# Streaming the high and low halves of the activations in one 512-column matmul, with groups of two channel tiles, in a one-core hybrid decoder layer

## The chip, the cores and the metric

The program runs on one core of a Trainium2 chip. The metric is device time of one launch in microseconds. The kernel before takes 532.43 us, the median of three runs that lie between 532.12 and 532.71 us.

## What is computed

One layer of a decoder for 256 tokens of width 2048, in float32:

```
h = rms_norm(x);  p = h @ w_in          # w_in is 2048 x 6408
A: RG-LRU (512 channels): conv4, gates, h_t = a_t h_{t-1} + u_t, times silu(lru_z)
B: mLSTM (768 channels): conv4, silu, block-diagonal q/k/v, gated scores, layer norm, times silu(ml_z)
C: attention (768 channels, 6 heads of 128, one causal block, ALiBi), times silu(mo_z)
x = x + concat(A, B, C) @ w_out
x = x + cross_attention(rms_norm(x), rms_norm(mem)) @ xa_wo      # 4 heads of 128
out = rms_norm(x)
```

## The kernel before

**The big products as split products.** `w_in`, `w_out`, `xa_wkv`, `xa_wq` and `xa_wo` come through one stream of 172 chunks, numbered from 0 (`CHUNKS`). A chunk is 128 partitions by up to 1024 columns of weights (512 KB). `load` (L151) brings it into one of four `raw` buffers, and `split` (L166) makes of it a high part `wh` on ACT (a copy that rounds to fp32r, L188) and a low part `wl` on DVE (raw minus high, L139), each in six buffers. The activations have a high and a low part too, in separate tiles `ah` and `al` (L196). A product is three fp32r matmuls: high by high, high by low, low by high.

**Groups.** `GROUPS` (L42) lists the passes over the contraction (16 tiles of 128). A group of kind `W` keeps weights stationary and streams 256 token columns; its result is [channel, token], two channel tiles side by side in each of two PSUM banks, so four channel tiles in a group. A chunk of it has two contraction tiles by four channel tiles, so 8 pairs of three matmuls:

```
 250 P.matmul(o, h[:, sl], mv_h, start=first and m % 2 == 0, stop=False, ...)
 251 P.matmul(o, h[:, sl], mv_l, start=False, stop=False, ...)
 253     P.matmul(o, l[:, sl], mv_h, start=False, stop=last, ...)
```

Kind `X` keeps activations stationary and streams 384 to 512 weight columns (L265 to L267). PSUM holds four accumulator banks (two groups) and four `ps` banks for all other matmuls.

**The order of the work** is written out (L1009 on). For chunk i the program first splits up to chunk i + 4 (`SPLIT_AHEAD`), then issues `mm(i)`, and when i ends a group calls `done` (L958), and then takes one `step` (L925) from a queue of generators. `done` puts the read-out of the finished accumulators at the head of the queue (`urgent`) and longer work at its end (`bg`): the recurrence (`lru_core`, L421), the mLSTM convolution (`ml_conv`, L486), gates, heads (L581) and layer norm (`ml_norm`, L636), and the attention heads (`mo_heads`, L697). Each engine runs its instructions in program order, so a read-out that waits for PE also holds the splits queued behind it on its engine, and each urgent read-out takes the step of one chunk from the work behind it. The step after chunk i stands on DVE and ACT just ahead of the split of chunk i + 5.

**Read-outs.** A bank holds two channel tiles. `silu_evac` (L458) multiplies the bank by the row of inverse norms on DVE and applies Silu on ACT; `u_evac` (L479), `qk_evac` (L684) and `ck_evac` (L800) are the multiplication alone, and `cq_evac` (L806) two ACT copies.

**Places that the prediction speaks of.** Chunks 16 to 23 are group `u1` (the last two tiles of u, the first two of lru_z), 24 to 39 are `o0` and `o1` (kind `X`), 40 to 79 are `q0`, `q1`, `k0`, `k1`, `z0`, 80 to 95 are `v0`, `v1` (kind `X`), 96 to 107 are `z1`, `z2`, 108 to 139 the output projection, 140 to 155 `ck` and `cq`, 156 to 163 `cv`. In `lru_core` the gate matmuls are L432 and L433, their sigmoids L434 and L435, the Exp and Tanh of the decays L440 and L441, the square root L448, the scan L454. In `ml_norm` the statistics are L642 and L643, the power on POOL L646, the scaling L652, the transposes on PE L660.

Of the kernel before, what the change touches and what calls it, by code (L numbers as in the profile page):

```python
# [18 lines left out]
NK = D // 128  # L19
# [7 lines left out]
# column offsets in w_in  # L27
# [10 lines left out]
def _t(off, *tiles):  # L38
# [22 lines left out]
    ("ck", "xa_wkv", "W", "m", _cols(0, 128, 256, 384)),  # L61
    ("cq", "xa_wq", "W", "h", _cols(0, 128, 256, 384)),
# [7 lines left out]
# per-partition vectors: name -> columns  # L70
# [27 lines left out]
def kernel(ctx: ExitStack, tc: tile.TileContext, xT, memT, x, mem, ws, vec_d, lw_d, fg_d, out):  # L98
# [16 lines left out]
    # ------------------------------------------------------------------ helpers  # L115
# [28 lines left out]
    # ------------------------------------------------------------------ weight stream  # L144
# [21 lines left out]
    def split(i, part=(0, 1)):  # L166
# [14 lines left out]
        elif GROUPS[g][0] == "cq":  # L181
            for kk in range(2):
                sl = slice(kk * n, (kk + 1) * n)
                gk = vc("xa_g", 2 * j + kk)
                S.activation(h[:, sl], r[:, sl], AF.Copy, scale=gk)
                stt(l[:, sl], r[:, sl], gk, h[:, sl].bitcast(F32), OP.mult, OP.subtract)
# [5 lines left out]
    # ------------------------------------------------------------------ activations  # L192
    act_hi = {"x": [None] * 8, "y": [None] * 8, "m": [None] * 8, "h": [None] * 8, "c": [None] * 2}
    act_lo = {"x": [None] * 8, "y": [None] * 8, "m": [None] * 8, "h": [None] * 8, "c": [None] * 2}

    def act_pair(which, j):  # L196
        tag = "y" if which in "ym" else "x"
        h = acts.tile([128, 512], F32R, tag="h" + tag, name=f"ah_{which}{j}")
        l = acts.tile([128, 512], F32R, tag="l" + tag, name=f"al_{which}{j}")
        act_hi[which][j], act_lo[which][j] = h, l  # L200
        return h, l
# [23 lines left out]
    def split_pair(which, j, src):
        """hi and lo of a [128, 512] float32 pair of contraction tiles."""
        h, l = act_pair(which, j)
        S.activation(h, src, AF.Copy)
        tt(l, src, h.bitcast(F32), OP.subtract)

    # ------------------------------------------------------------------ matmuls of the stream
    acc = {}

    def mm(i):
# [6 lines left out]
        for kk in range(kc):  # L241
            k = kc * j + kk
            xh, xl = act_hi[act][k // 2], act_lo[act][k // 2]
            first, last, b = k == 0, k == NK - 1, k % 2 * 256
            if kind == "W":
                mv_h, mv_l = xh[:, b:b + 256], xl[:, b:b + 256]
# [11 lines left out]
            else:  # L258
                mh, ml = h[:, kk * n:kk * n + n], l[:, kk * n:kk * n + n]
                for t in range(2):  # L260
# [3 lines left out]
                    sl = slice(b + t * 128, b + t * 128 + 128)  # L264
# [4 lines left out]
        if name == "cv" and j == 7:  # L269
            for t in range(2):  # L270
                for kk in range(2):
                    sl = slice(kk * 256 + t * 128, kk * 256 + t * 128 + 128)
                    P.matmul(a[t], xh[:, sl], h[:, kk * n:kk * n + n], start=False, stop=False)
                    P.matmul(a[t], xh[:, sl], l[:, kk * n:kk * n + n], start=False, stop=False)
                    P.matmul(a[t], xl[:, sl], h[:, kk * n:kk * n + n], start=False, stop=kk == 1)

    # ------------------------------------------------------------------ start: loads and constants
# [37 lines left out]
    def late_consts():  # L315
# [5 lines left out]
        # the product of the q and k blocks, transposed: the sum over o of wq[c, o] wk[d, o]  # L321
# [14 lines left out]
    def rstd_of(out_t, ssq, n, eps):  # L336
        """out = (ssq / n + eps) ** -0.5"""
# [4 lines left out]
    def log1p(out_t, e, name):  # L342
        """log(1 + e) for 0 <= e <= 1 as 2 artanh(e / (2 + e))"""
# [25 lines left out]
    # ------------------------------------------------------------------ row statistics  # L369
# [4 lines left out]
    def square(which, j):  # L374
        """adds the squares of a pair of staged contraction tiles to the running sum"""
# [34 lines left out]
    # ------------------------------------------------------------------ RG-LRU  # L410
# [51 lines left out]
    def lru_z(a, b, c):  # L462
        if c == 0:
            L["sz"] = big(1, 4, 256)
        silu_evac(L["sz"][:, c:c + 2, :], a, b)
        yield
# [9 lines left out]
    # ------------------------------------------------------------------ mLSTM  # L476
    M = {}

    def u_evac(a, b, c):  # L479
# [3 lines left out]
        tt(M["u"][:, c:c + 2, 3:259], bank(a, b), rb("x"), OP.mult)  # L483
# [182 lines left out]
    def ml_z(a, b, c):  # L666
        if c == 0:
            M["sz"] = big(6, 6, 256)
        silu_evac(M["sz"][:, c:c + 2, :], a, b)
        yield  # L670
# [10 lines left out]
    # ------------------------------------------------------------------ MoBA: one causal block  # L681
    B = {}

    def qk_evac(which, tag, a, b, c):  # L684
        if c == 0:
            B[which] = big(tag, 6, 256)
        tt(B[which][:, c:c + 2, :], bank(a, b), rb("x"), OP.mult)
# [75 lines left out]
    # ------------------------------------------------------------------ residual and norm before cross-attention  # L763
# [36 lines left out]
    def ck_evac(a):  # L800
        C["k"] = big(1, 4, 256)
        for b in range(2):
            tt(C["k"][:, 2 * b:2 * b + 2, :], bank(a, b), rb("m"), OP.mult)
        yield

    def cq_evac(a):  # L806
        qT = big(2, 4, 256)
        for b in range(2):
            S.activation(qT[:, 2 * b:2 * b + 2, :], bank(a, b), AF.Copy)
# [32 lines left out]

    def cv_out(a):
# [9 lines left out]
        for t in range(2):  # L853
# [4 lines left out]
            oh, ol = act_pair("c", t)  # L858
# [5 lines left out]
    # ------------------------------------------------------------------ output projection and final norm  # L864
# [247 lines left out]
```

## Time and profile before

| what | value |
|---|---|
| median of the timed runs | 532.43 us (532.12 to 532.71) |
| profiled execution, first to last instruction (its own time; the page gives no other) | 530.7 us |
| what lies around that span in the timed runs | 1.7 us (532.43 - 530.7) |
| PE, PEld busy | 519.7 and 486.1 us |
| DVE, ACT, POOL busy | 339.3, 281.4 and 49.7 us |
| DMA | 96.73 MB, 182 GB/s |

How to read it: PE is the matmul side of the tensor engine and PEld its weight loads, which overlap. A matmul's listed duration contains its way through the pipeline, so that matmuls overlap in the records; what one costs in a stream is the distance from its start to the next one's start. The chain of work that ended last follows the end of the kernel back to what released each step.

### The profile page before, as it was taken

The numbers are of one execution on the slowest core, as the hardware profiler recorded it, in microseconds if no ns is written. First come the engines' busy times: TensorE is split into PE (matmuls) and PEld (weight loads), VectorE is DVE, ScalarE is ACT, GpSimd is POOL, SyncE is SP. The second block draws the span as 40 slices with busy tenths as digits, with TensorE's granted clock in tenths as the row PEclk, the third lists the DMA queues.
The fourth block names the chain that finished last, engine by engine and source line by source line (L and its number), as shares of the span: only waits on it lengthen the run. The fifth ranks groups of instructions, "written<-read, shape, count | busy, mean of one in ns | idle before, by whom it ended". The sixth has DMA issues, their size and how long they took to land.

```text
span 530.7 us, 8855 instructions
## 1 busy us (share of the span) xinstructions
PE 519.7 (98%) x3498; PEld 486.1 (92%) x3498; DVE 339.3 (64%) x520; ACT 281.4 (53%) x419; POOL 49.7 (9%) x62
## 2 busy tenths in 40 slices
PE   8999999999999999999999999999999999999993
PEld 6999999999998889999999999888888899998883
DVE  6986927794576435466657667665667875437574
ACT  5964477577644232342456455553657665347343
POOL 7462000200000000000200000000051110000000
PEclk9999999999999999999999999999999999999997
DMA  8985535468455445535367335688685555633604
GB/s 286 357 262 178 149 113 174 127 201 269 136 185 162 131 143 165 160 100 178 120 186 255 116 120 167 200 298 278 215 286 184 171 189 190 207 117 115 220 24 158
DMA packets 30362, 96.73 MB, mean 182 GB/s; under 512 B 3312, under 2 KB 3696, under 8 KB 30320
## 3 DMA queue, kind: packets, MB, share of 16 engines
q1 hardware_dynamic: 30176, 96.02, 55.3%
q8 instruction: 27, 0.44, 0.3%
q14 instruction: 15, 0.12, 0.1%
q10 hardware_dynamic: 144, 0.14, 0.1%
HBM read 94.05 MB, written 2.10 MB: 181 GB/s over the span
## 4 chain that ended last, share of the span: by engine, by line
PE 93%; issue 2%; DMA 2%; DVE 2%; SPq 0%; ACT 0%; ACTq 0%; POOLq 0%; POOL 0%; DVEq 0%
PE acc_out L265 6%; PE acc_out L267 5%; PE acc_out L266 5%; PE acc_z L253 4%; PE acc_z L251 4%; PE acc_z L250 4%; PE acc_k L250 3%; PE acc_q L250 3%; PE acc_u L250 3%; PE acc_u L253 3%; PE acc_u L251 3%; PE acc_k L251 3%; PE acc_q L251 3%; PE acc_q L253 3%; PE acc_k L253 3%; PE acc_o L266 2%
## 5 line engine op out<-in xcount | busy, mean ns | idle before, releaser
L139 DVE TENSOR_TENSOR wl<-raw,wh 128x1024 fp32r<-128x1024 f32 (+3 forms) x166 | 197.9, 1203 | 100.0 <-ACT wh L188 99.2
L188 ACT ACTIVATE wh<-raw 128x1024 fp32r<-128x1024 f32 (+2 forms) x162 | 161.1, 1010 | 55.5 <-PE acc_k L251 12.8
L265 PE MATMUL acc_out<-wh,ah_y 128*128 128x512 f32 x128 | 50.8, 397 | 0.0
L267 PE MATMUL acc_out<-wh,al_y 128*128 128x512 f32 x128 | 49.9, 390 | 0.0
L266 PE MATMUL acc_out<-wl,ah_y 128*128 128x512 f32 x128 | 49.8, 389 | 0.0
L250 PE MATMUL acc_z<-ah_x,wh 128*128 128x256 f32 x160 | 46.6, 291 | 0.0
L253 PE MATMUL acc_z<-ah_x,wl 128*128 128x256 f32 x160 | 45.2, 283 | 0.0
L251 PE MATMUL acc_z<-al_x,wh 128*128 128x256 f32 x160 | 45.2, 283 | 0.0
L250 PE MATMUL acc_q<-ah_x,wh 128*128 128x256 f32 x128 | 37.2, 291 | 0.0
L250 PE MATMUL acc_k<-ah_x,wh 128*128 128x256 f32 x128 | 37.0, 289 | 0.0
L250 PE MATMUL acc_u<-ah_x,wh 128*128 128x256 f32 x128 | 36.8, 288 | 0.0
L383 POOL TENSOR_TENSOR mask<-mask,yt 128x512 f32<-128x512 f32 x14 | 22.3, 1594 | 150.7 <-ACT yt L382 150.7
L253 PE MATMUL acc_u<-ah_x,wl 128*128 128x256 f32 x128 | 36.2, 283 | 0.0
L251 PE MATMUL acc_k<-al_x,wh 128*128 128x256 f32 x128 | 36.2, 283 | 0.0
L251 PE MATMUL acc_u<-al_x,wh 128*128 128x256 f32 x128 | 36.2, 283 | 0.0
L253 PE MATMUL acc_q<-ah_x,wl 128*128 128x256 f32 x128 | 36.2, 283 | 0.0
L251 PE MATMUL acc_q<-al_x,wh 128*128 128x256 f32 x128 | 36.2, 283 | 0.0
L253 PE MATMUL acc_k<-ah_x,wl 128*128 128x256 f32 x128 | 36.2, 283 | 0.0
L251 PEld LDWEIGHTS acc_z<-al_x,wh 128*128 128x128 f32 x160 | 30.6, 192 | 0.2
L250 PEld LDWEIGHTS acc_z<-ah_x,wh 128*128 128x128 f32 x160 | 30.6, 192 | 0.2
L253 PEld LDWEIGHTS acc_z<-ah_x,wl 128*128 128x128 f32 x160 | 30.6, 191 | 0.0
L267 PEld LDWEIGHTS acc_out<-wh,al_y 128*128 128x128 f32 x128 | 24.0, 188 | 5.1
(282 smaller groups left out, 1294.5 us busy)
## 6 DMA issues: line engine op xcount, KB each, us to landing
raw<-ws SPq DMA_DIRECT2D x138, 512.0 KB, 4.2
raw<-ws SPq DMA_DIRECT2D x24, 384.0 KB, 3.1
raw<-ws SPq DMA_DIRECT2D x8, 392.0 KB, 3.1
w<-x SPq DMA_DIRECT2D x4, 512.0 KB, 6.6
w<-memT SPq DMA_DIRECT2D x8, 256.0 KB, 4.7
out<-xg SPq DMA_DIRECT2D x8, 256.0 KB, 3.0
w<-xT SPq DMA_DIRECT2D x7, 256.0 KB, 6.0
raw<-ws SPq DMA_DIRECT2D x4, 256.0 KB, 4.8
```

The lines of the kernel that those rows point to most:

```text
L139: V.tensor_tensor(out, a, b, op)
L188: S.activation(h[:, :kc * n], r[:, :kc * n], AF.Copy)
L250: P.matmul(o, h[:, sl], mv_h, start=first and m % 2 == 0, stop=False, skip_group_check=True)
L251: P.matmul(o, h[:, sl], mv_l, start=False, stop=False, skip_group_check=True)
L253: P.matmul(o, l[:, sl], mv_h, start=False, stop=last, skip_group_check=True)
L265: P.matmul(o, xh[:, sl], mh, start=first, stop=False)
L266: P.matmul(o, xh[:, sl], ml, start=False, stop=False)
L267: P.matmul(o, xl[:, sl], mh, start=False, stop=last)
L383: G.tensor_tensor(sq[which], sq[which], q, OP.add)
```

## The change

The groups of kind `W` behind `u0` become kind `C`, with two channel tiles each. The high and low halves of an activation tile lie side by side in one tile, so the high weights stream both in one matmul of 512 columns, and the low weights stream the high half alone. One channel tile fills a bank: its left half is the sum of high by high and low by high, its right half high by low. The halves are added when the bank is read: `fold` reads two banks into `ev` (DVE, or ACT for cq) and adds the halves on DVE, or on POOL for q and k.

```diff
-    ("u1", "w_in", "W", "x", _cols(*_t(O_U, 4, 5), *_t(O_LZ, 0, 1))),
+    ("u4", "w_in", "C", "x", _cols(*_t(O_U, 4, 5))),
+    ("lz0", "w_in", "C", "x", _cols(*_t(O_LZ, 0, 1))),
     ("o0", ...), ("o1", ...)
-    q0 (lz 2,3 and q 0,1), q1, k0, k1 (k 4,5 and z 0,1), z0: W, four tiles each
+    lz2, q0, q2, q4, k0, k2, k4, z0, z2, z4: C, two tiles each
     ("v0", ...), ("v1", ...)
-    z1 (four tiles of mo_z), z2 (two), later ck, cq (four each): W
+    mz0, mz2, mz4, later ck0, ck2, cq0, cq2: C, two tiles each
```
```diff
+            if kind == "C":
+                both = act_all[act][k // 2][:, k % 2, :, :].rearrange("p a b -> p (a b)")
+                for m in range(2):
+                    sl = slice(kk * n + m * 128, kk * n + m * 128 + 128)
+                    P.matmul(a[m], h[:, sl], both, start=first, stop=False, skip_group_check=True)
+                    P.matmul(a[m][:, :256], l[:, sl], xh, start=False, stop=last, skip_group_check=True)
...
+    def fold(dst, a, eng, which=None):
+        e = small("ev", 2, 2, 256)
+        for m in range(2):
+            if which is None:
+                S.activation(e[:, m, :, :], bank(a, m), AF.Copy)
+            else:
+                tt(e[:, m, :, :], bank(a, m), rb(which), OP.mult)
+        eng.tensor_tensor(dst, e[:, :, 0, :], e[:, :, 1, :], OP.add)
...
-    def silu_evac(dst, a, b):
-        tt(dst, bank(a, b), rb("x"), OP.mult)
+    def silu_evac(dst, a):
+        fold(dst, a, V, "x")
         S.activation(dst, dst, AF.Silu)
...
-        elif GROUPS[g][0] == "cq":
-            for kk in range(2):
+        elif GROUPS[g][0].startswith("cq"):
+            for kk in range(kc):
```

A chunk of a `C` group has four contraction tiles by two channel tiles, so again 8 pairs and again 512 KB, and chunk numbers keep their meaning: the channels come in the same order. `done` is called after every fourth chunk in these groups, once where it was called for two read-outs after every eighth. Queue order of the longer work stays.

The change moves instructions on ACT and DVE. **ACT, around chunks 25 to 29** (`wh25` is the high part of chunk 25, `w5` and `w6` the decays of the recurrence, `w1` the gate lru_z), before and then after:

```order
L188 ACTIVATE wh26_1014<-raw26_866 128x784
L440 ACTIVATE w5_1008<-w3_926,nsp8_119 128x256
L441 ACTIVATE w6_1009<-w3_926,sp8_118 128x256
L440 ACTIVATE w5_1008<-w3_926,nsp8_119 128x256
L441 ACTIVATE w6_1009<-w3_926,sp8_118 128x256
L188 ACTIVATE wh27_1048<-raw27_900 128x784
L188 ACTIVATE wh28_1079<-raw28_942 128x784
L460 ACT_TABLE_LOAD
L460 ACTIVATE w1_1099<-w1_1099 128x512
L188 ACTIVATE wh29_1102<-raw29_982 128x784
```
```order
L199 ACTIVATE wh27_986<-raw27_868 128x784
L490 ACT_TABLE_LOAD
L490 ACTIVATE w1_1008<-w1_1008 128x512
L199 ACTIVATE wh28_1014<-raw28_894 128x784
L470 ACT_TABLE_LOAD
L470 ACTIVATE w5_980<-w3_914,nsp8_119 128x256
L471 ACTIVATE w6_981<-w3_914,sp8_118 128x256
L470 ACTIVATE w5_980<-w3_914,nsp8_119 128x256
L471 ACTIVATE w6_981<-w3_914,sp8_118 128x256
L199 ACTIVATE wh29_1038<-raw29_930 128x784
```

The second half of the decays moved from ahead of `wh27` to behind the Silu, with a table load of its own; the Silu moved ahead of `wh28`.

**DVE, around chunks 83 to 86** (`acc_z` and `ev` are the gate of the mLSTM, `ml_st` and `ml_mv` the statistics of its norm), before and then after; before, these four pairs of statistics stand ahead of `wl82`:

```order
L139 TENSOR_TENSOR wl83_2829<-raw83_2686,wh83_2828 128x768
L139 TENSOR_TENSOR w6_2607<-acc_z00_2581,rrow_663 128x512
L139 TENSOR_TENSOR wl84_2861<-raw84_2716,wh84_2860 128x768
L139 TENSOR_TENSOR w6_2607<-acc_z01_2582,rrow_663 128x512
L139 TENSOR_TENSOR wl85_2883<-raw85_2746,wh85_2882 128x768
L645 TENSOR_SCALAR ml_rs_2773<-ml_mv_2772 128x8
```
```order
L150 TENSOR_TENSOR ev_2499<-acc_z40_2401,rrow_655 128x512
L150 TENSOR_TENSOR ev_2499<-acc_z41_2402,rrow_655 128x512
L438 TENSOR_TENSOR w6_2279<-ev_2499 128x512
L150 TENSOR_TENSOR wl84_2505<-raw84_2399,wh84_2504 128x768
L675 BN_STATS ml_st_2524<-w3_1806 128x6
L676 BN_AGGR ml_mv_2463<-ml_st_2524 128x2
...
L150 TENSOR_TENSOR wl85_2537<-raw85_2423,wh85_2536 128x768
L678 TENSOR_SCALAR ml_rs_2464<-ml_mv_2463 128x8
```

Two read-outs of one instruction each became one of three, and four pairs of statistics moved behind it.

**ACT, around chunks 103 and 104** (`mo_p` are transposed probabilities, `mo_l` logits of an attention head, `w2` the gate mo_z), after; before, the same place has no Silu and no table load:

```order
L199 ACTIVATE wh103_2989<-raw103_2844 128x1024
L490 ACT_TABLE_LOAD
L490 ACTIVATE w2_3011<-w2_3011 128x512
L199 ACTIVATE wh104_3017<-raw104_2864 128x1024
L762 ACTIVATE mo_p1_3045<-ps36_3041 128x384
L750 ACT_TABLE_LOAD
L750 ACTIVATE mo_l0_3050,mo_sm0_3053<-mo_l0_3050,mo_mx0_3052 128x128
```

A read-out of the gate moved in between the third and the fourth attention head; before it came behind the sixth.

## Rows read from the trace of the kernel before

**Rows 1.** The page: part 1 (busy us, share of the span, instructions), and part 4 (the chain that ended last, by engine).

```profile
PE 519.7 (98%) x3498; PEld 486.1 (92%) x3498; DVE 339.3 (64%) x520; ACT 281.4 (53%) x419; POOL 49.7 (9%) x62
...
PE 93%; issue 2%; DMA 2%; DVE 2%; SPq 0%; ACT 0%; ACTq 0%; POOLq 0%; POOL 0%; DVEq 0%
```

**Rows 2.** Timeline of PE over group cq, its first and last matmul, and the first of cv (start us, us, engine, line, operation, out<-in, shapes). From the first row to the last are 192 matmuls of 256 columns (8 chunks of 24).

```profile
446.56 0.28 PE L250 MATMUL acc_cq<-ah_h,wh 128*128 128x256 f32 x1
...
469.48 0.28 PE L253 MATMUL acc_cq<-ah_h,wl 128*128 128x256 f32 x1
469.60 0.40 PE L265 MATMUL acc_cv<-wh,ah_m 128*128 128x512 f32 x1
```

**Rows 3.** Timeline of PE in out1, the starts of two chunks with 36 matmuls of 512 columns from the one to the other (3 chunks of 12), and at the end of out3, where a matmul of 512 columns is followed by one of 256 (columns as in rows 2).

```profile
365.41 0.39 PE L265 MATMUL acc_out<-wh,ah_y 128*128 128x512 f32 x1
...
373.57 0.39 PE L265 MATMUL acc_out<-wh,ah_y 128*128 128x512 f32 x1
...
422.44 0.39 PE L267 MATMUL acc_out<-wh,al_y 128*128 128x512 f32 x1
422.67 0.28 PE L250 MATMUL acc_ck<-ah_m,wh 128*128 128x256 f32 x1
```

**Rows 4.** Groups of instructions by line and shape (line engine op out<-in shapes xcount | busy us, mean ns | idle us before them, what ended it).

```profile
L139 DVE TENSOR_TENSOR w<-acc_z,rrow 128x512 f32<-128x512 f32 x5 | 3.4, 687 | 3.1 <-PE acc_z L253 3.1
L139 DVE TENSOR_TENSOR xg<-w,w 128x512 f32<-128x512 f32 x7 | 4.8, 690 | 0.2
L460 ACT ACTIVATE w<-w 128x512 f32<-128x512 f32 x8 | 5.1, 632 | 19.4 <-DVE w L139 19.4
L383 POOL TENSOR_TENSOR mask<-mask,yt 128x512 f32<-128x512 f32 x14 | 22.3, 1594 | 150.7 <-ACT yt L382 150.7
L188 ACT ACTIVATE wh<-raw 128x1024 fp32r<-128x1024 f32 x130 | 134.8, 1052 | 47.2 <-PE acc_k L251 12.8 <-DMA raw<-ws 11.0 <-issue 8.5
L142 DVE SCALAR_TENSOR_TENSOR al_m<-w,vec,ah_m 128x256 fp32r<-128x256 f32 x16 | 7.5, 510 | 0.6 <-ACT ah_m L222 0.4
```

**Rows 5.** Timelines of ACT, then of DVE, around the end of u1 (in brackets the idle time ahead of a row and what ended it).

```profile
72.54 0.47 ACT L434 ACTIVATE w<-ps,vec 128x256 f32<-128x256 f32 x1 [2.15 <-PE ps L433]
74.13 0.86 ACT L188 ACTIVATE wh<-raw 128x784 fp32r<-128x784 f32 x1
75.00 1.28 ACT L440 ACT_TABLE_LOAD   x1
...
77.91 0.84 ACT L188 ACTIVATE wh<-raw 128x784 fp32r<-128x784 f32 x1
...
84.23 0.63 ACT L460 ACTIVATE w<-w 128x512 f32<-128x512 f32 x1 [1.08 <-DVE w L139]
...
81.14 0.98 DVE L139 TENSOR_TENSOR wl<-raw,wh 128x784 fp32r<-128x784 f32 x1 [1.37 <-ACT wh L188]
82.03 0.68 DVE L139 TENSOR_TENSOR w<-acc_u,rrow 128x512 f32<-128x512 f32 x1
...
85.64 0.98 DVE L139 TENSOR_TENSOR wl<-raw,wh 128x784 fp32r<-128x784 f32 x1 [1.45 <-ACT wh L188]
86.54 1.22 DVE L139 TENSOR_TENSOR w<-w 128x1024 f32<-128x1024 f32 x1
```

**Rows 6.** Timelines at the end of o0 and o1: ACT's wait for DVE, DVE's wait for ACT behind it, the low part of chunk 40 on DVE, and its first use on PE.

```profile
101.89 1.28 ACT L506 ACT_TABLE_LOAD   x1 [6.14 <-DVE if L142]
...
105.00 0.96 DVE L139 TENSOR_TENSOR wl<-raw,wh 128x768 fp32r<-128x768 f32 x1 [3.06 <-ACT wh L188]
...
114.24 1.22 DVE L139 TENSOR_TENSOR wl<-raw,wh 128x1024 fp32r<-128x1024 f32 x1
...
115.82 0.28 PE L253 MATMUL acc_q<-ah_x,wl 128*128 128x256 f32 x1
```

**Rows 7.** Timelines around chunks 79 to 85: DVE (statistics, read-out of the gate, power, scaling), POOL, and PE (transposes of the norm, and what follows them).

```profile
242.77 0.35 DVE L642 BATCH_NORM_STATS2 ml_st<-w 128x6 f32<-128x192 f32 x1
...
245.10 0.96 DVE L139 TENSOR_TENSOR wl<-raw,wh 128x768 fp32r<-128x768 f32 x1
...
251.89 0.69 DVE L139 TENSOR_TENSOR w<-acc_z,rrow 128x512 f32<-128x512 f32 x1 [2.62 <-PE acc_z L253]
...
260.46 1.51 DVE L652 TENSOR_SCALAR w<-w,ml_mv,ml_rs 128x192 f32<-128x192 f32 x4 [1.55 <-POOL ml_rs L646]
...
258.13 2.29 POOL L646 TENSOR_TENSOR ml_rs<-ml_rs,half 128x8 f32<-128x8 f32 x1 [160.16 <-DVE ml_rs L645]
...
262.81 0.98 PE L660 MATMUL ps<-ident,w 128*128 128x128 f32 x4
263.56 0.42 PE L265 MATMUL acc_v<-wh,ah_x 128*128 128x384 f32 x1
```

**Rows 8.** Timelines in the attention heads: PE transposes the probabilities of the fourth head; DVE scales them (two instructions), and splits chunk 104 next.

```profile
310.28 0.49 PE L727 MATMUL ps<-ident,mo_l 128*128 128x128 f32 x3
...
307.63 0.55 DVE L721 TENSOR_SCALAR mo_l<-mo_l,mo_sm 128x128 f32<-128x128 f32 x2
308.38 1.23 DVE L139 TENSOR_TENSOR wl<-raw,wh 128x1024 fp32r<-128x1024 f32 x1 [0.20 <-ACT wh L188]
```

**Rows 9.** Timelines at the end of cq: ACT's two copies of the accumulators, and PE's first score matmuls behind the first chunk of cv.

```profile
469.08 1.32 ACT L809 ACTIVATE w<-acc_cq 128x512 f32<-128x512 f32 x2 [4.10 <-PE acc_cq L253]
...
472.35 0.81 PE L821 MATMUL ps<-w,w 128*128 128x256 f32 x3
```

More of the change, by code (lines that the diff above doesn't have):

```diff
@@ L60 @@
     ("out3", "w_out", "X", "y", [(1536, 512)]),
-    ("ck", "xa_wkv", "W", "m", _cols(0, 128, 256, 384)),
-    ("cq", "xa_wq", "W", "h", _cols(0, 128, 256, 384)),
+    ("ck0", "xa_wkv", "C", "m", _cols(0, 128)),
+    ("ck2", "xa_wkv", "C", "m", _cols(256, 384)),
+    ("cq0", "xa_wq", "C", "h", _cols(0, 128)),
+    ("cq2", "xa_wq", "C", "h", _cols(256, 384)),
     ("cv", "xa_wkv", "X", "m", [(512, 512)]),
@@ L194 @@
     act_lo = {"x": [None] * 8, "y": [None] * 8, "m": [None] * 8, "h": [None] * 8, "c": [None] * 2}
+    act_all = {"x": [None] * 8, "y": [None] * 8, "m": [None] * 8, "h": [None] * 8, "c": [None] * 2}
     def act_pair(which, j):
[L197 to L201, printed above, removed]
+        a = acts.tile([128, 2, 2, 256], F32R, tag="y" if which in "ym" else "x", name=f"a_{which}{j}")
+        act_all[which][j] = a
+        act_hi[which][j], act_lo[which][j] = a[:, :, 0, :], a[:, :, 1, :]
+        return act_hi[which][j], act_lo[which][j]
     staged = {}
@@ L242, in mm @@
             k = kc * j + kk
[L243 to L246, printed above, removed]
+            xh, xl = act_hi[act][k // 2][:, k % 2, :], act_lo[act][k // 2][:, k % 2, :]
+            first, last = k == 0, k == NK - 1
+            if kind == "C":
[4 more added lines that the diff above has]
+                    P.matmul(a[m][:, :256], l[:, sl], xh, start=False, stop=last, skip_group_check=True)
+            elif kind == "W":
+                mv_h, mv_l = xh, xl
                 for m in range(n // 128):
@@ L482, in u_evac @@
             V.memset(M["u"][:, :, 0:3], 0.0)
-        tt(M["u"][:, c:c + 2, 3:259], bank(a, b), rb("x"), OP.mult)
+        if c < 4:
+            tt(M["u"][:, c:c + 2, 3:259], bank(a, c // 2), rb("x"), OP.mult)
+        else:
+            fold(M["u"][:, c:c + 2, 3:259], a, V, "x")
         yield
@@ L664, in ml_norm, with ml_z @@
             yield
-    def ml_z(a, b, c):
+    def ml_z(a, c):
         if c == 0:
             M["sz"] = big(6, 6, 256)
-        silu_evac(M["sz"][:, c:c + 2, :], a, b)
-        yield
+        yield from silu_evac(M["sz"][:, c:c + 2, :], a)
     def ml_y():
@@ L682, with qk_evac @@
     B = {}
-    def qk_evac(which, tag, a, b, c):
+    def qk_evac(which, tag, a, c):
         if c == 0:
             B[which] = big(tag, 6, 256)
-        tt(B[which][:, c:c + 2, :], bank(a, b), rb("x"), OP.mult)
+        fold(B[which][:, c:c + 2, :], a, G, "x")
         yield
@@ L747, in mo_heads, with mo_z @@
             yield
-    def mo_z(a, b, c):
+    def mo_z(a, c):
         if c == 0:
             B["sz"] = big(2, 6, 256)
-        silu_evac(B["sz"][:, c:c + 2, :], a, b)
-        yield
+        yield from silu_evac(B["sz"][:, c:c + 2, :], a)
     def mo_y(j0, j1):
@@ L798, with ck_evac, cq_evac @@
     C = {}
[L800 to L803, printed above, removed]
-        yield
[L806 to L809, printed above, removed]
+    def ck_evac(a, c):
+        if c == 0:
+            C["k"] = big(1, 4, 256)
+        dst = C["k"][:, c:c + 2, :]
+        fold(dst, a, V, "m")
+        yield
+    def cq_evac(a, c):
+        if c == 0:
+            C["q"] = big(2, 4, 256)
+        qT = C["q"]
+        fold(qT[:, c:c + 2, :], a, V)
+        if c == 0:
+            yield
+            return
         sc, nsc = small("ca_sc", 2), small("ca_nsc", 2)
@@ L841, in cq_evac, with c_pair @@
             yield
+    def c_pair(t):
+        a = acts.tile([128, 2, 2, 256], F32R, tag="x", name=f"a_c{t}")
+        return a[:, 0, :, :], a[:, 1, :, :]
     def cv_out(a):
@@ L876, in wo_unit @@
         w = 512 // parts
-        xg = acts.tile([128, 512], F32, tag="hy", name=f"xg{g}{t}")
+        xg = acts.tile([128, 2, 2, 256], F32, tag="y", name=f"xg{g}{t}")
+        xg = xg.rearrange("p a b c -> p (a b c)")[:, :512]
         XG[g, t] = xg
@@ L961, in done @@
         elif name == "u0":
-            urgent(u_evac(a, 0, 0), u_evac(a, 1, 2))
-        elif name == "u1":
-            urgent(u_evac(a, 0, 4), lru_z(a, 1, 0))
+            urgent(u_evac(a, 0), u_evac(a, 2))
+        elif name == "u4":
+            urgent(u_evac(a, 4))
             bg(ml_conv(), ml_qkv())
+        elif name == "lz0":
+            urgent(lru_z(a, 0))
         elif name == "o0":
```

97 lines of the change are left out of this document (52 added, 45 removed).

## The prediction

> **What bounds the kernel now.** I read the page first: in the chain of work that ended last, PE has 93% of the span, and it is busy 98% of it, while DVE has 64% and ACT 53% [rows 1]. So time is won by fewer or closer matmuls, and lost where PE waits. Second, the timeline of PE, for the price of a matmul in a stream: from the first matmul of cq to the first of cv, 192 matmuls of 256 columns take 469.60 - 446.56 = 23.04 us, 120.0 ns each [rows 2]; 36 matmuls of 512 columns take 373.57 - 365.41 = 8.16 us, 226.7 ns each [rows 3]. The reader is to see that the second is less than twice the first: 256 more columns cost 106.7 ns, so 13.3 ns of either price is fixed. Third, the timelines of DVE and ACT, for how far the low parts of the weights are ahead of PE. At one place they are hardly ahead: the low part of chunk 40 is finished at 114.24 + 1.22 = 115.46 us and first used at 115.82 [rows 6], a lead of 0.36 us. Whatever delays DVE by more than that ahead of chunk 40 makes PE wait.
>
> **Matmuls.** 76 chunks become kind C (8 of u4 and lz0, 16 of lz2 to q4, 16 of k0 to z0, 8 of z2 and z4, 12 of mz, 16 of ck and cq), each with 8 pairs of a contraction tile and a channel tile: 608 pairs. A pair was 3 x 120.0 = 360.0 ns and becomes 226.7 + 120.0 = 346.7 ns, if the two widths keep their prices in turn. One transition of each kind stands in the trace: a 256 behind a 512 starts after 0.23 us, a 512 behind a 256 after 0.12 us [rows 2, 3]. Gain: 608 x 13.3 ns = **8.1 us**; a chunk goes from 2.880 to 2.773 us. Of it 0.85 us lies ahead of chunk 40 and 7.25 us behind.
>
> The Trainium skill, "TensorE: Matmul & The Clock Gate", section "Back-to-back issue gap", speaks against this: a matmul of N columns takes N / 2.4 + 2.5 ns at the full clock, so the fixed part that a merged matmul saves is 2.5 ns, and 608 of them give an estimate of 1.5 us. By that rule the sum below would be 5.0 us slower, 537.4 us. The trace has 13.3 ns, and it decides.
>
> **Read-outs.** A read-out of two channel tiles was one DVE instruction, 0.69 us; a fold is two of these and an add, which I price at the 0.69 us of an add from SBUF [rows 4]. With starts 0.60 us apart where nothing is waited for, a fold takes 0.60 + 0.72 + 0.69 = 2.0 us. Eleven folds with the add on DVE, six without and two adds for cq put 11 x 1.38 + 6 x 0.69 + 2 x 0.69 = 20.7 us on DVE, which has 191 us free. The work as such is hidden; what counts is where a fold stands in a chain that PE waits for. I found three such places.
>
> **First place, chunks 23 to 40.** Before, the read-out of u1 was two steps behind the end of the group; now u4 takes the step of chunk 19 and lz0 that of chunk 23, so the two gate units of the recurrence, its decays and all behind them move on by one step up to chunk 24. Step by step [rows 5]: the second gate unit comes after chunk 21 in place of 20, so 2.77 us later less 5 x 0.106, or 2.24 us. ACT starts its sigmoids at 72.54 + 2.24 and, after the high part of chunk 26, a table load and the first half of the decays, is at the high part of chunk 27 at 77.91 + 2.24 = 80.15. DVE makes its low part from 81.03 (the ACT instruction is 0.84) and starts the fold 0.89 later, 81.92, about when it did the first read-out before (82.03); PE has finished by then. Fold to 83.93; Silu (0.63) to 84.6; then ACT has the high part of chunk 28 to 85.35, a table load (1.28) to 86.64, the second half of the decays (77.91 - 76.28 = 1.63) and the high part of chunk 29 to 89.10. DVE starts the low part of chunk 29 at 89.14, where it was 85.64: **3.5 us later**. From there to chunk 40 the order is the old one, and I take it as one chain: the two long waits in it are of ACT for DVE (6.14 us) and at once of DVE for ACT (3.06 us), not for PE [rows 6]. So the low part of chunk 40 comes at 118.96, 3.14 us later than its first use before. Against a PE that is 0.85 us earlier and a use at 114.97, the stall is 118.96 - 114.97 = **4.0 us**. Bounds: 0, if the chain has slack that the rows don't show; 4.9, the shift and PE's own gain without the lead and another 0.5 for joints.
>
> **Second place, the norm of the mLSTM.** At the end of chunk 79 DVE waited for PE and read the gate in two steps, with Silu and the high part of the next chunk behind each; now one fold stands there, and four pairs of statistics, which before lay ahead of chunk 82, stand behind chunk 84. The first bank is finished 0.37 us nearer to the end of the chunk, since its last matmuls are now followed by two rather than six. From the end of chunk 79, at 252.41: before, the scaling starts at 260.46, 8.05 us behind it [rows 7]. Now: fold to 1.86, Silu to 2.53, high and low part of chunk 84 to 3.26 and 4.26, four pairs of statistics (245.10 - 242.77 = 2.33) to 6.5, low part of chunk 85 to 7.46, 0.09 more, then POOL's power (2.29) and the scaling at 9.96. So it is 1.9 us later, and PE's transposes waited for it already: four of them took from 262.81 to 263.56, 0.75 us [rows 7]. Stall: **1.9 us**, bounds 1.0 and 2.5.
>
> **Third place, the attention heads.** The read-out of mz0 comes between the third and fourth head. Ahead of the fourth head DVE and ACT get a fold (2.0), Silu (0.66), the high part (1.05 less 0.10 of overlap) and low part (1.23 less 0.08) of chunk 104 [rows 4, 8]: 4.75 us. The two table loads hide while ACT waits for DVE. PE needs the fourth head's probabilities 310.28 - 308.18 = 2.1 us after they are ready [rows 8], and comes to them one chunk later, less six chunks' gain: 2.77 - 0.64 = 2.1. Stall: 4.75 - 4.2 = **0.55 us**, bounds 0 and 3.1 (below).
>
> **At no cost.** POOL's six adds (about 1.6 us each [rows 4]): q and k are read by the heads from chunk 96 on, 17 chunks or more behind the last but one; if POOL slowed DVE there, the lead would pay. The finer split of cq: 4 x 0.51 = 2.04 us of DVE a chunk [rows 4], below PE's 2.77. The read-out of cq2: two ACT copies from 469.45 (0.37 later) to 470.77 and an add to 471.5, while PE gets to the scores at 472.35 [rows 9]; with that cover gone it costs 0.7. Loads: same bytes in the same chunks.
>
> **Sum.** -8.1 + 4.0 + 1.9 + 0.55 = -1.65 us. The profiled execution's 530.7 us become 529.05; with the 1.7 us that lie around the span in the timed runs, 532.43 becomes **530.8 us**. I count a change as measurable from 0.2%, 1.06 us: below 531.4 is faster, above 533.5 slower.
>
> **Rivals.**
> - The cover holds. If none of the three chains reaches PE, all 8.1 us are won: 524.3 us. For it speak the long waits inside the first chain [rows 6]; against it, that each is ended by the other engine's last instruction. Chance 0.08. If one of the two larger stalls fails to come, 526.8 or 528.9 us: 0.12.
> - The attention heads give back more (the other side). If DVE and ACT never regain their lead, the first read-out costs a fold, Silu and both table loads, 2.0 + 0.63 + 2.56 = 5.2, less the lead of 2.1: 3.1 us in place of 0.55, and mz2's read-out behind the sixth head the same. 533.3 us with the first alone, 535.9 with both, slower. It decides from the point where a head's probabilities are over 2.1 us late. For it: DVE goes from a unit straight to a split with 0.20 us of idle time [rows 8]; against it: the read-out takes a step, so PE has a chunk without head matmuls. Chance 0.17, half for each.
> - The pace is not what it seems. If the fixed part stays with the pair (a 512 in turn with a 256 takes 240 ns), nothing is won and the stalls of 6.45 us remain: 538.9 us. The two transitions in the trace speak against it [rows 2, 3]; the skill's 2.5 ns, above, would come close to it. Chance 0.04.
> - Further hand-offs of this sort that I didn't see, around 533 us: 0.05.
>
> **How the numbers follow.** The forecast, its three stalls within their bounds, has 0.54; its own range is 529.0 to 532.3, and about two thirds of it lie below 531.4. Faster: 0.36 + 0.08 + 0.12 = 0.56. Same: 0.15 of the forecast and 0.05 of the rest. Slower: 0.24. The range leaves out the full gain (0.08), both read-outs of the heads (0.08) and the failing pace (0.04): 526.0 to 533.8 us.
>
> **What would show it.** Right: starts of matmuls in q, k, z and mz at 0.227 and 0.120 us in turn, 2.77 us a chunk; PE waiting for DVE's low parts from chunk 34 on, some 4 us in all before chunk 41; transposes of the norm spread over 2.7 us; DVE busy near 360 us. Wrong: pairs at 0.36 us; no wait of PE between 100 and 125 us; or over 2 us of waiting in the attention heads.

## The result: slower by 1.1%, and the profile after

| what | before | after |
|---|---|---|
| median of four runs | 532.57 us (532.12 to 532.74) | 539.12 us (536.02 to 540.18) |
| ratio | | 1.0114, 95% interval 1.0084 to 1.0145 |
| profiled execution: its own time, its span | (not on the page), 530.7 us | 538.4, 536.6 us |

The prediction said 530.8 us, faster; it was wrong in sign. The median moved by 6.5 us, the profiled spans by 5.9. The page after, part 1 and the chain that ended last, against [rows 1]:

```profile
PE 518.2 (97%) x2890; PEld 453.9 (85%) x2890; DVE 366.6 (68%) x566; ACT 287.0 (53%) x439; POOL 62.3 (12%) x68
...
PE 72%; issue 12%; DVE 8%; ACT 4%; DMA 1%; POOL 1%; SPq 0%; ACTq 0%; POOLq 0%; DVEq 0%
```

PE has 608 matmuls fewer and almost the same busy time, and DVE now has 8% of the chain. Where PE waits, the view of its waits tells (who <- for whom: us in total, times, longest). Before:

```profile
PE ps L294 <- DVE half L334: 1.3, 1, 1.3
PE acc_lx L253 <- DVE wl L139: 1.2, 2, 0.7
PE acc_lx L250 <- ACT wh L179: 0.3, 1, 0.3
```

After, the rows that are new (at the start of the kernel one wait grew from 0.3 to 1.0 us and one of 0.3 us is new; they are not shown):

```profile
PE ps L693 <- DVE w L685: 1.9, 1, 1.9
PE ps L759 <- ACT mo_p L762: 1.5, 1, 1.5
...
PE acc_o L284 <- ACT wh L199: 1.1, 1, 1.1
...
PE acc_o L285 <- DVE wl L150: 0.9, 2, 0.6
PE ps L740 <- DVE w L770: 0.7, 1, 0.7
PE ps L740 <- ACT mo_p L762: 0.4, 1, 0.4
```

Before, PE waited only in the first 15 us; now it waits at the three forecast places: chunks 34 to 40 (L284, L285), the norm (L693), the heads (L759, L740). The view counts only what lies behind a matmul's listed end, and at the first place that is 2.0 us of the 4.15 that PE lost there. So their size comes from the start of each chunk's first matmul in the two traces, after minus before:

| stretch | forecast, us | measured, us | how |
|---|---|---|---|
| start of the kernel | 0 | +0.34 | at chunk 8 |
| pace of 76 chunks | -8.1 | -5.1 | -0.57 from chunk 16 to 24, -2.86 from 41 to 80, -0.83 from 140 to 156; 63 chunks, 0.068 each, and the same taken for chunk 40 and the 12 of mz |
| first place | +4.0 | +4.15 | from -0.25 at chunk 34 to +3.83 at 41, and 0.07 of pace |
| norm, wait | +1.9 | +1.87 | from 0.98 at chunk 84 to 2.85 at 85 |
| norm, clock | none | +1.58 | from 2.85 at chunk 85 to 4.43 at 86 |
| heads | +0.55 | +3.13 | from 4.39 at chunk 96 to 6.71 at 108, and 0.81 of pace |
| sum | -1.65 | +5.97 | spans: +5.9 |

**Pace.** Timeline of PE: first matmuls of chunks 49 and 50, then of cq and cv, against [rows 2]:

```profile
147.14 0.39 PE L262 MATMUL acc_q<-a_x,wh 128*128 128x512 f32 x1
...
149.92 0.39 PE L262 MATMUL acc_q<-a_x,wh 128*128 128x512 f32 x1
...
452.85 0.40 PE L262 MATMUL acc_cq<-a_h,wh 128*128 128x512 f32 x1
...
475.46 0.40 PE L284 MATMUL acc_cv<-wh,a_m 128*128 128x512 f32 x1
```

The first stretch is 8 pairs in 2.78 us, 347 ns each, as forecast; the second is 64 pairs in 22.61 us, 353.3 ns each. Pairs come in one of two patterns: near 347 ns on the mean (346 and 347, or 343 and 350), or 349, 350 and 361 in turn. A pattern stays until other matmuls come between, and 47 of the 76 chunks ran in the slower one.

**First place.** Timelines of ACT, DVE and PE, against [rows 5, 6]:

```profile
84.58 0.63 ACT L490 ACTIVATE w<-w 128x512 f32<-128x512 f32 x1 [1.67 <-DVE w L438]
...
85.98 1.28 ACT L470 ACT_TABLE_LOAD   x1
...
89.76 0.98 DVE L150 TENSOR_TENSOR wl<-raw,wh 128x784 fp32r<-128x784 f32 x1 [2.80 <-ACT wh L199]
...
109.14 0.44 PE L284 MATMUL acc_o<-wh,a_x 128*128 128x384 f32 x1 [1.08 <-ACT wh L199]
110.13 0.44 PE L285 MATMUL acc_o<-wl,a_x 128*128 128x384 f32 x1 [0.55 <-DVE wl L150]
```

The low part of chunk 29 starts at 89.76; the forecast of 89.14 and the late start of 0.34 make 89.48. Six chunks on, PE waits, mostly for low parts, as forecast; its longest single wait, 1.08 us, is for a high part from ACT.

**Norm.** DVE's scaling, PE's transposes and what follows, then the windows of that stretch (us; busy us of PE, PEld, DVE, ACT, POOL; granted clock; DMA share, GB/s), against [rows 7]:

```profile
263.32 1.50 DVE L685 TENSOR_SCALAR w<-w,ml_mv,ml_rs 128x192 f32<-128x192 f32 x4 [1.56 <-POOL ml_rs L679]
...
263.79 0.30 PE L693 MATMUL ps<-ident,w 128*128 128x128 f32 x1
266.04 0.62 PE L693 MATMUL ps<-ident,w 128*128 128x128 f32 x3 [1.95 <-DVE w L685]
...
267.32 0.52 PE L285 MATMUL acc_v<-wl,a_x 128*128 128x384 f32 x1
267.64 0.52 PE L286 MATMUL acc_v<-wh,a_x 128*128 128x384 f32 x1
```

```profile
263.00:266.00 3.00, 1.09 (x7) 0.78 (x5) 2.68 (x7) 0.00 (x0) 1.57 (x5) 1.00 0.49 166
266.00:269.00 3.00, 2.96 (x13) 2.88 (x14) 2.42 (x5) 1.57 (x3) 0.00 (x0) 0.68 0.52 145
269.00:272.00 3.00, 3.00 (x16) 2.90 (x15) 0.25 (x1) 1.19 (x3) 0.00 (x0) 0.75 0.76 229
```

Behind the wait a matmul of 384 columns costs 0.32 us, from start to start, in place of 0.173 (2.08 us for the 12 of a chunk): the clock was at 1.2 GHz from 267.1 to 270.5 us. In the trace of before it is at 2.4 GHz until 525.0 us.

**Heads.** ACT's first exponentials of the third and the fourth head before, then the same two after, with the table load ahead of the second of them; DVE's logits and scaling of the fourth head, and PE's three waits, against [rows 8]:

```profile
301.81 0.40 ACT L718 ACTIVATE mo_l<-mo_l,mo_mx 128x128 f32<-128x128 f32 x1 [2.23 <-DVE mo_mx L716]
...
306.41 0.40 ACT L718 ACTIVATE mo_l<-mo_l,mo_mx 128x128 f32<-128x128 f32 x1 [2.29 <-DVE mo_mx L716]
```

```profile
306.12 0.40 ACT L750 ACTIVATE mo_l<-mo_l,mo_mx 128x128 f32<-128x128 f32 x1 [2.23 <-DVE mo_mx L748]
...
315.50 1.28 ACT L750 ACT_TABLE_LOAD   x1 [2.27 <-DVE mo_mx L748]
316.79 0.40 ACT L750 ACTIVATE mo_l<-mo_l,mo_mx 128x128 f32<-128x128 f32 x1
...
314.02 0.55 DVE L153 SCALAR_TENSOR_TENSOR mo_l<-mask,ps 128x384 f32<-128x384 f32 x1
...
318.01 0.55 DVE L753 TENSOR_SCALAR mo_l<-mo_l,mo_sm 128x128 f32<-128x128 f32 x2
...
313.37 0.46 PE L740 MATMUL ps<-w,w 128*128 128x128 f32 x2 [0.37 <-ACT mo_p L762]
...
319.15 0.55 PE L759 MATMUL ps<-ident,mo_l 128*128 128x128 f32 x3 [1.46 <-ACT mo_p L762]
320.37 0.49 PE L740 MATMUL ps<-w,w 128*128 128x128 f32 x2 [0.67 <-DVE w L770]
```

From one head's exponentials to the next it was 4.60 us and is 10.67, so 6.07 later, where the forecast had 4.75. This table load stands behind the wait for DVE, not in it, so its 1.28 us are open, and they are nearly all of that difference. The first and third of PE's waits are of another kind: for a `ps` bank that ACT (mo_p, behind a split) or DVE (a copy, behind a split) has yet to read.

### The profile page after: what moved, and what is told of

It is laid out like the page before. It is cut to its first block, busy times and chain, and to the rows that moved or that the text cites. A ratio compares the mean times of both kernels' runs of the same rounds, so it can differ in the third digit from the quotient of the medians.

```text
span 536.6 us, 7728 instructions
## 1 busy us (share of the span) xinstructions
PE 518.2 (97%) x2890; PEld 453.9 (85%) x2890; DVE 366.6 (68%) x566; ACT 287.0 (53%) x439; POOL 62.3 (12%) x68
## 4 chain that ended last, share of the span: by engine, by line
PE 72%; issue 12%; DVE 8%; ACT 4%; DMA 1%; POOL 1%; SPq 0%; ACTq 0%; POOLq 0%; DVEq 0%
PE acc_out L284 5%; PE acc_out L286 5%; PE acc_out L285 5%; PE acc_k L262 4%; PE acc_q L262 4%; DVE wl L150 3%; PE acc_cq L262 3%; PE acc_ck L262 3%; PE acc_q L263 2%; PE acc_k L263 2%; PE acc_mz L262 2%; PE acc_lz L262 2%; ACT wh L199 2%; PE acc_v L285 2%; PE acc_v L286 2%
## 5 line engine op out<-in xcount | busy, mean ns | idle before, releaser
L284 PE MATMUL acc_out<-wh,a_y 128*128 128x512 f32 x128 | 50.8, 397 | 0.0
L286 PE MATMUL acc_out<-wh,a_y 128*128 128x512 f32 x128 | 49.9, 390 | 0.0
L285 PE MATMUL acc_out<-wl,a_y 128*128 128x512 f32 x128 | 49.8, 389 | 0.0
L262 PE MATMUL acc_mz<-a_x,wh 128*128 128x512 f32 x96 | 35.4, 409 | 0.0
L262 PE MATMUL acc_k<-a_x,wh 128*128 128x512 f32 x96 | 34.6, 402 | 0.0
L262 PE MATMUL acc_q<-a_x,wh 128*128 128x512 f32 x96 | 34.2, 399 | 0.0
L262 PE MATMUL acc_z<-a_x,wh 128*128 128x512 f32 x96 | 34.1, 399 | 0.0
L286 PEld LDWEIGHTS acc_out<-wh,a_y 128*128 128x128 f32 x128 | 24.0, 188 | 5.2
L285 PEld LDWEIGHTS acc_out<-wl,a_y 128*128 128x128 f32 x128 | 24.1, 188 | 4.7
L284 PEld LDWEIGHTS acc_out<-wh,a_y 128*128 128x128 f32 x128 | 24.0, 188 | 4.7
L263 PE MATMUL acc_z<-a_x,wl 128*128 128x256 f32 x96 | 26.9, 281 | 0.0
L263 PE MATMUL acc_k<-a_x,wl 128*128 128x256 f32 x96 | 26.9, 280 | 0.0
L263 PE MATMUL acc_mz<-a_x,wl 128*128 128x256 f32 x96 | 26.8, 279 | 0.0
L285 PE MATMUL acc_o<-wl,a_x 128*128 128x392 f32 (+1 forms) x64 | 22.3, 349 | 0.9 <-DVE wl L150 0.9
L284 PE MATMUL acc_o<-wh,a_x 128*128 128x392 f32 (+1 forms) x64 | 21.7, 340 | 1.1 <-ACT wh L199 1.1
```

Source lines behind the costliest of these rows:

```text
L262: P.matmul(a[m], h[:, sl], both, start=first, stop=False, skip_group_check=True)
L263: P.matmul(a[m][:, :256], l[:, sl], xh, start=False, stop=last, skip_group_check=True)
L284: P.matmul(o, xh[:, sl], mh, start=first, stop=False)
L285: P.matmul(o, xh[:, sl], ml, start=False, stop=False)
L286: P.matmul(o, xl[:, sl], mh, start=False, stop=last)
```

## The experiments

Theory A: the loss lies at three places, where a read-out stands ahead of something that PE waits for. Theory B: DVE and ACT carry too much work as a whole. Times are medians of each set of runs; before was 532.1 to 532.4 us beside them.

### One part back at a time

Edits in `GROUPS` (with the read-outs of before for these groups):

```diff
-    u4 and lz0: C                 +    u1: W, four tiles        (e1, e4)
-    z2 and z4: C                  +    z2: W, four tiles        (e2, e4)
-    mz0, mz2, mz4: C              +    mz0, mz4: W, 4 + 2 tiles (e3, e4)
```

e1. 

> The changed kernel with the last u and first lru_z tiles again one group W of four. Theory A (three places, each a fold that stands ahead of something PE waits for): the wait of PE at chunks 34 to 41 (4.1 us) goes, the pace of 8 chunks is given back (+0.55 us), the waits in the norm and the heads stay: 539.1 - 4.1 + 0.55 = 535.5 us. Theory B (DVE is late as a whole by its 27 us of added work, and PE waits wherever the cover is thinnest): the wait moves to a later place and the kernel stays at 538 us or more.

Measured 534.32 us (531.9 to 536.35), 1.2 us less than theory A gave: the 4 us went. The norm's wait (1.89 us here) and the three of the heads stayed. The profiled execution, the fastest, kept the full clock behind the norm's wait; in it chunk 86 came no later than chunk 85, against before.

e2. 

> The changed kernel with the last four mLSTM gate tiles again one group W. Theory A: the four pairs of statistics stand ahead of chunk 82's split again, the wait of PE in the norm (1.9 us) goes, and with it the stretch at 1.2 GHz behind it (1.6 us); the pace of 8 chunks is given back (+0.4 us): 539.1 - 1.9 - 1.6 + 0.4 = 536.0 us, granted clock 1.00 from 260 to 275 us. Theory B: the transposes of the norm still wait, since DVE is late as a whole: 538.5 us. A third: if the clock falls for another reason than the wait of PE ahead of it, it falls again without that wait: 537.6 us.

Measured 536.47 us (534.96 to 537.17). No wait and no fall at the norm. But now the clock fell at the first place, which had waits in the changed kernel too, yet no fall in its trace:

```profile
108.00:111.00 3.00, 2.05 (x8) 1.80 (x9) 2.56 (x5) 3.00 (x6) 0.00 (x0) 0.88 0.18 46
111.00:114.00 3.00, 3.00 (x11) 3.00 (x11) 2.93 (x6) 2.87 (x5) 0.00 (x0) 0.55 0.78 264
```

e3. 

> The changed kernel with mo_z again groups W of four and two tiles. Theory A: no read-out stands between the third and fourth attention head, PE's three waits there (together about 3.3 us of 312 to 321 us) go, the pace of 12 chunks is given back (+1.0 us): 539.1 - 3.3 + 1.0 = 536.8 us. Theory B: 538.5 us, with waits of PE in the heads or in the first chunks of the output projection.

Measured 534.49 us (533.7 to 536.65), 2.3 us better than expected; no wait in the heads, none later. Its trace also has a fall at the first place (110.9 to 114.3 us), and none at the norm, where PE waited 1.95 us as in the changed kernel.

e4. 

> The changed kernel with all three parts back at W; kind C stays for lz2 to z0 and for ck and cq, 48 chunks. Theory A: the effects add up: no wait of PE over 0.6 us behind chunk 16, no fall of the clock ahead of the end, runs within 0.7 us of each other; 48 chunks at 0.07 us less each and 0.3 us of a later start against the kernel before: 532.6 - 3.4 + 0.3 = 529.5 us. Theory B: less than the sum, 532 to 533 us, with the wait elsewhere.

Measured 529.19 us (528.72 to 529.56), ratio to before 0.994 (0.9928 to 0.9953). Theory A gave 529.5, B 532 or more. No wait of PE behind 20 us, no fall of the clock, and the spread of 4 us is 0.8. So the three parts back make a change that is slower by 1.1% one that is faster by 0.6%, with 48 of its chunks and 12 of its 19 folds left.

### The pace

```diff
 e5, per contraction tile:  512(m0) 256(m0) 512(m1) 256(m1)  ->  512(m0) 512(m1) 256(m0) 256(m1)
 e6, per chunk:             the eight of 512 columns first, then the eight of 256
```

e5. 

> The kernel of the run with all three parts back at W (529.2 us), and in its 48 chunks of kind C the two matmuls of 512 columns of a contraction tile first, then the two of 256. In that run 30 of the 48 chunks ran at 353.3 ns a pair, in a pattern that repeats after three pairs, the others at 346.7. Theory P (the extra belongs to the turn from one width to the other): half the turns, half of 30 x 53 ns: -0.8 us, 528.4 us. Theory Q (it belongs to something else that each matmul or each weight load has): 529.2 us.

e6. 

> The same, with all eight matmuls of 512 columns of a chunk first and then all eight of 256: two turns a chunk. Theory P: every chunk at 2.77 us, 30 x 53 ns won: 527.6 us. Theory Q: 529.2 us. The low part of a chunk is first used 1.6 us later here, which wins nothing where PE does not wait for it, and in that run it did not.

Measured 528.03 (527.88 to 528.72) and 528.24 us (527.88 to 528.51): both about 1 us below e4. The order of the widths does set the pace, but not in proportion to the turns: a quarter of the turns wins no more than half. In e6, timeline of PE (merged rows), first matmuls of cq and of cv:

```profile
443.14 2.00 PE L259 MATMUL acc_cq<-a_h,wh 128*128 128x512 f32 x8
...
465.49 0.40 PE L280 MATMUL acc_cv<-wh,a_m 128*128 128x512 f32 x1
```

64 pairs in 22.35 us are 349.2 ns each, against 353.3; in e5 the same 64 take 22.29 us, 348.3 each. The 346.7 of the sum of prices is not reached over this group in either. What makes the slow pattern stays open.

### All of kind C, three read-outs put off

```diff
-            urgent(lru_z(a, 0))              +            later(1, lru_z(a, 0))
-            urgent(ml_z(a, 4))               +            later(4, ml_z(a, 4))
-            urgent(mo_z(a, 0))               +            later(3, mo_z(a, 0))
+    def later(n, *gens):                     # n steps of the work at the head of the queue first
```

e7. 

> The changed kernel with every group of kind C kept and only three read-outs put off: that of lz0 by one step (behind the second half of the decays), that of z4 by four (behind statistics, power and scaling), that of mz0 by three (behind the sixth head). Theory A (the place of a fold is what costs, not the fold): the waits in the norm and in the heads go, of the 4.1 us ahead of chunk 41 at most 1.3 stay (the fold's extra DVE time), no fall of the clock; 532.1 - 5.9 of pace + 1.0 = 527.2 us. Theory B (the folds' work as such): 532 us or more.

e8. 

> Both: every group of kind C, the three read-outs put off, and in a chunk all matmuls of 512 columns first. Theory A with P: 47 chunks x 53 ns less than the run before: 527.2 - 2.5 = 524.7 us. Theory A with Q: 527.2 us.

Measured 535.77 (534.65 to 536.47) and 534.69 us (534.01 to 534.98): misses of 8.6 and, against A with P, 10.0 us, for the most part for a reason that neither theory had. The norm's wait went, as A said. At the first place 2.7 us stayed in e7, twice what I allowed; I put them down to two folds, u4's and lz0's, of 1.3 us extra each, which no run separates. At the third, e7's PE timeline:

```profile
318.80 0.79 PE L262 MATMUL acc_mz<-a_x,wh 128*128 128x512 f32 x1 [3.58 <-DVE ev L150]
```

Chunk 104 needs the banks of mz0, and put off behind the sixth head they were read too late. A group of two tiles gives its banks four chunks of rest where one of four tiles gave eight; so a read-out can't be put off far. And the clock was at 1.2 GHz from 317.3 us, while PE still waited, to 324.1. Windows of e7:

```profile
315.00:318.00 3.00, 0.22 (x2) 0.00 (x0) 1.80 (x4) 2.98 (x6) 0.00 (x0) 0.88 0.26 107
318.00:321.00 3.00, 2.20 (x7) 1.91 (x8) 2.03 (x4) 1.08 (x3) 0.00 (x0) 0.50 0.53 175
321.00:324.00 3.00, 3.00 (x11) 2.52 (x11) 2.29 (x3) 0.68 (x1) 0.00 (x0) 0.50 0.04 15
```

### The clock

The 3.5 us of standing still, filled (e8 is the kernel it is compared with):

```diff
+        if name == "mz4" and j == 0:
+            p = ps()
+            for _ in range(15):
+                P.matmul(p, act_hi["x"][0][:, 0, 0:128], both, start=True, stop=True)
```

e11. 

> The run in which PE waited 3.5 us for the accumulator of mz0 ahead of chunk 104 and the granted clock was 0.5 for 6.8 us from then on (534.7 us), with 15 matmuls of 512 columns more ahead of chunk 104 (into a free bank, never read; 15 x 0.227 = 3.4 us, which is the length of the wait). Theory C (the clock falls because PE stands still): the wait is filled, the clock stays at 1.0, chunk 104 takes 2.8 us in place of 5.3: 534.7 - 2.5 = 532.2 us. Theory D (it falls for another reason): 534.7 us, and the 0.5 stays in the record.

Measured 532.12 us (531.45 to 532.76), 2.6 below e8, whose granted clock in the three windows shown for e7 is 0.87, 0.50 and 0.50. The same windows in e11:

```profile
315.00:318.00 3.00, 2.84 (x12) 1.83 (x11) 2.76 (x5) 1.56 (x2) 0.00 (x0) 1.00 0.16 37
318.00:321.00 3.00, 3.00 (x18) 2.63 (x18) 1.35 (x2) 1.58 (x2) 0.00 (x0) 1.00 0.37 138
321.00:324.00 3.00, 3.00 (x20) 2.67 (x19) 2.22 (x4) 0.71 (x2) 0.00 (x0) 1.00 0.54 168
```

More work on PE made the kernel faster: standing still lowered the clock, and that cost more than the work that prevented it. The Trainium skill, "TensorE: Matmul & The Clock Gate", section "HAM oscillation — how this bites in real kernels", says that a PE that waits for its data is throttled and then starts its next work at the lower clock; these runs agree, with 0.50 against 1.00 for the same 6 us. What PE waited for here was the read-out of an accumulator.

### The heads: the fold, or what hangs on it

```diff
 e9 (on e4, mz of kind C):  read-out of mz0 in its old place, but only the fold
+        if c == 2:  # in the read-out of mz2, as a step of its own; in e13 and e14 in the same step
+            S.activation(B["sz"][:, 0:2, :], B["sz"][:, 0:2, :], AF.Silu)
 e10: u1 of kind W, all else C, order of e6, z4 put off by four, mz0's Silu put off
 e12: as e10, u4 and lz0 of kind C too (adds on POOL, lz0 put off by one); low parts last in X chunks too
 e13, e14: e10 and e12 with the two Silus in one step
```

e9. 

> The kernel with all three parts back at W (529.2 us), but mo_z again kind C with its read-out in the old place between the third and fourth attention head, and only the Silu of mz0 put off, to behind that of mz2. In the changed kernel this read-out held DVE for 3.65 us (a fold of 2.0 and 1.64 of waiting for ACT behind the Silu) and ACT's next exponentials for another 1.28 us (table load). Theory H (hand-over and table loads cost, the fold does not): DVE is held for 2.0 us, less than the 4.2 us that PE's order allows; the waits in the heads fall from 3.3 to 0.3 us or less, the pace of 12 chunks is won: 529.2 - 1.0 + 0.3 = 528.5 us. Theory F (the fold's own 2.0 us): the waits stay, 531 to 531.5 us.

Measured 530.43 us (529.63 to 530.71), 1.9 above what theory H gave for the whole. It holds for the heads: the trace has no wait of PE in them, with the fold where it was. But chunk 116, with the first transposes of the output projection, took 3.83 us in place of 3.08, and PE waited 0.8 us for the low part of chunk 144. The Silu in a step of its own had moved all longer work on by a chunk.

e10. 

> A version meant to be faster than both: u1 at W, all else of kind C, in a chunk all matmuls of 512 columns first, the read-out of z4 put off by four steps, the Silu of mz0 put off. From 528.1 us (eight and eight, with W for z and mo_z): pace of 8 and of 12 chunks at up to 0.107 us each, -0.9 and -1.3; 0.3 us in the heads: 526.2 us. If the heads' waits stay: 529 us.

e12. 

> Every group of kind C as in the change, with: lz0's read-out put off by one step and the adds of u4 and lz0 on POOL, z4's put off by four, the Silu of mz0 put off, and the matmuls on the low part last in every chunk of kind C and X. With the read-out of lz0 put off, 2.6 us of waiting were left ahead of chunk 41, which is two folds' extra time on DVE (2 x 1.3). The adds on POOL take 2 x 0.69 of it, the later use of the low part about 1.2 us more: near nothing left. Against the run meant to be fastest: pace of 8 chunks won, -0.6 us; POOL's adds last 1.6 to 2.2 us, and if the Silu behind them holds ACT, +1: 525.6 to 527.2 us.

Measured 527.81 (526.98 to 528.48) and 527.62 us (527.27 to 528.45), 1.6 above e10's forecast and 0.4 above the upper end of e12's, both with the same delay behind the heads (chunk 116 takes 3.96 and 3.87 us). In e12 the first place costs 0.4 us.

e13. 

> The version meant to be fastest (527.8 us), but the put-off Silu of mz0 in the same step as mz2's read-out. There it took a step of its own, so all longer work behind it came one chunk later, and PE lost 1.5 us behind the heads: 0.7 us at chunks 109 to 111 (values of the heads' end), 0.9 at the first transposes of the output projection; 1.2 us where it waited for the low part of chunk 144. Theory S (the step's place in the queue is the cause): these waits go, 527.8 - 1.5 = 526.3 us. Theory W (the Silu's and the fold's work is the cause): 527.8 us.

e14. 

> The same edit in the version with every group of kind C (527.6 us), where PE lost 1.9 us behind the heads: Theory S: 526.0 us; Theory W: 527.6 us.

Measured 526.78 (526.32 to 527.09) and 526.48 us (526.08 to 526.94): 1.0 and 1.1 us less for nearly the same work in one step fewer (the two Silus also changed places). Chunk 116 is back at 3.08 us. Theory S holds, with a smaller gain than the 1.5 us expected: the 0.7 us at chunks 109 to 111 were no loss. In e12 chunks 108 and 109 hold eight matmuls of the heads, in e14 four, the others being done before; from chunk 96 to 112 the two take 54.52 and 54.48 us.

e14 has every group of kind C that the change has, as many folds, and is faster than before: ratio 0.9893 (0.9876 to 0.9909). Its waits of PE, all of them in the first 20 us:

```profile
PE ps L325 <- DVE half L365: 1.3, 1, 1.3
PE acc_lx L271 <- DVE wl L150: 0.9, 2, 0.7
PE acc_lx L268 <- ACT wh L190: 0.3, 1, 0.3
```

and part 1 of its page, with DVE nearly as busy as in the changed kernel:

```profile
PE 513.8 (98%) x2890; PEld 453.8 (87%) x2890; DVE 363.3 (69%) x564; ACT 282.1 (54%) x436; POOL 65.2 (12%) x70
```

This speaks against B as it was put: with DVE 363.3 us busy in place of 366.6, and all 19 folds, PE waits nowhere behind 15 us. It does not show that the place of a read-out is all. e14 also uses the low parts later in a chunk and has two adds of the first place on POOL, and there the place alone gave back 1.5 of 4.15 us (e7); the rest went, all but 0.4, only with those edits (e12), which no run separates.

## Why the prediction was wrong

- **What bounds it** (PE, with a thin cover ahead of chunk 40): right, and all three places were named. Two were right in size: 4.15 us for 4.0, and 1.87 for 1.9. e1 and e2 show that they belong to these parts. Of the prediction's own signs of being wrong one came: PE waits 2.5 us in the heads, over the 2 it named.
- **Matmuls**, "if the two widths keep their prices in turn": mis-sized. 29 of 76 chunks kept them; over all the gain was 5.1 us, not 8.1. I had two single transitions for the price of 608 pairs. e5 and e6 show that the order of the widths matters, not why. The rival in which nothing is gained gave 538.9 us, near the median, but for the wrong reason.
- **Third place**, "The two table loads hide while ACT waits for DVE": failed. The first hid; the second comes behind the wait in ACT's program and cost 1.28 us. A load behind its wait stood in [rows 6] already (1.28 us behind 6.14). And I looked only at when the probabilities were ready, not at the four `ps` banks, whose readers stand behind the same splits (waits of 0.37 and 0.67 us). Measured 3.13 us, the size of the rival "the heads give back more" (3.1), though for the first read-out alone and not by the same sum. e9 shows the Silu and its loads as the cause, and not the fold.
- **The sum** had no term for the clock: a wait was priced at its own length. In the profiled execution the norm's wait of 1.87 us was followed by a fall that cost 1.58 more. It does not follow each wait (the traces of e1 and e3 have the wait without the fall), and the four runs of the change lie 4 us apart, those of e4 0.8. That the slower ones spent more time at 1.2 GHz is likely from their mean clock (0.986 in two of them, 0.994 in the profiled one, 0.997 in the fastest); where they did is not known, for they have no trace. That standing still is the cause is shown for the wait of 3.5 us alone (e11).
- Together: 3.0 of pace, 2.6 in the heads, 1.6 of clock, 0.3 of a later start are the 7.6 us between -1.65 and +5.97. The start of chunk 1 differs by up to 0.9 us from before in traces of kernels that do the same there, so the last is no effect of the change.
- **At no cost** held for ck, cq and POOL's adds: PE does not wait there.

## What to carry to other kernels

When a tuned kernel is bound by one engine and the others run a chunk or two ahead, a smaller group can change more through the places of its read-outs than through their work: at the norm and in the heads the place, and what hangs on it, was nearly all of the loss, at the first place about a third (1.5 of 4.15 us). Go through each engine's program at every new read-out, with its table load, the buffers whose readers it holds up, and the steps that move behind it. A group half as large leaves its accumulator half the time until it is needed again. Price a wait of PE by more than its length where the clock can fall, and a new alternation of matmuls by a stretch that shows the alternation, not by single transitions.

## What the hardware showed that I had not expected

- Pairs of 512 and 256 columns in turn, each matmul with its own weights, ran at 1040 or at 1060 ns per three pairs, and changed between the two only where other matmuls came between.
- Waits of PE of 1 to 2 us were followed in some executions by a stretch at 1.2 GHz (267.1 to 270.5 us in the change, 110.3 to 113.7 in e2, 110.9 to 114.3 in e3), in others not (at the norm in e1 and e3); the one of 3.5 us in both traces that had it (e7, e8).
- Fifteen idle matmuls, 3.4 us of them in a wait of 3.5 us, saved 2.6 us.
